# Three feed-forward stages that begin with block products and a plain pair in place of a halved pair

## The chip, the cores and the metric

The kernel runs on one core of one Trainium2 chip. The metric is the device time of one execution in microseconds, lower is better; several executions are run and the median is given. The engines of the core are named as in the profile: PE is TensorE's matmul stream and PEld its weight loads, DVE is VectorE, ACT is ScalarE, POOL is GpSimd, and SP issues most of the transfers.

## The reference

A decoder trunk of two layers over 512 tokens of 1024 features, in float32. Each layer is a half-step feed-forward block, a token mixing block with three branches, and a second half-step feed-forward block, with a root-mean-square norm before and after each. The part that matters here is the feed-forward block, with 2816 hidden features (22 tiles of 128):

```python
def _swiglu(t, w_gate, w_up, w_down):
    return (jax.nn.silu(t @ w_gate) * (t @ w_up)) @ w_down

for l in range(DEPTH):
    f = _swiglu(_rmsnorm(h, ffn1_pre_g[l]), ffn1_w_gate[l], ffn1_w_up[l], ffn1_w_down[l])
    h = h + 0.5 * _rmsnorm(f, ffn1_post_g[l])
    ...
    f = _swiglu(_rmsnorm(h, ffn2_pre_g[l]), ffn2_w_gate[l], ffn2_w_up[l], ffn2_w_down[l])
    h = h + 0.5 * _rmsnorm(f, ffn2_post_g[l])
```

The mixing block also uses the memory, 256 rows of 1024 features, normed by the reciprocal root of each row's mean square.

## The kernel before

**Numbers in two parts.** Every float32 operand of a matmul is split into a high part (`h`, a cast on ScalarE, line 188 or 191) and a low part (`l`, the difference, on VectorE, line 189 or 192). `mm3` then issues three matmuls, high by high, high by low and low by high (lines 214 to 216). So every weight unit of 128 x 1024 elements per use costs one transfer of 512 KB, one cast and one subtraction.

**Stages.** There are four feed-forward stages, `a0`, `c0`, `a1` and `c1`, and between a and c of a layer stands the mixing. Stage `a0` takes the input `x`; the other three take the normed output of the stage before (`src` is b0, c0 and b1). 20 of the 22 hidden tiles are computed in five groups of four (`TG` = 0, 4, 8, 12, 16). A group's gate and up products over the two halves of the tokens and the two halves of the features are computed in a Strassen-like scheme of seven block products instead of eight, each over 128-token stationary blocks with 512 weight columns moving: 24 matmuls of 512 columns (`gate_up`). Products 0 and 1 (and 6) take parts of the normed input itself; 2 to 5 take sums over the halves of the tokens, which VectorE makes (`sums`). Products 0 and 1 need only the first half of the tokens. Group 0 runs in the order 0 to 6 (`FIRST`), the others in the order 0, 2, 3, 4, 5, 1, 6 (`ORDER`). The result of each product is accumulated in a bank and copied or added into a tile, and after product 6 two transposition steps (`feature_major`) turn the group's hidden features.

**The remaining pair.** Hidden tiles 20 and 21 (`EARLY`) are computed as an ordinary pair, gate and up, in the function `halved` (line 808): once over the first half of the tokens, 96 matmuls of 256 columns, and once over the second half, 96 more. A stage begins while the norm of its last two token tiles is still being computed. Therefore its jobs begin: half 0 of the pair, product 0 of group 0, half 1 of the pair, which waits for all tokens, and then products 1 to 6 of group 0, product 0 and 2 of group 4, the transpositions of group 0, and so on. Half 0 of the pair and product 0 cover the norm's last steps.

**The norm and the planner.** The jobs of TensorE are traced in the order of a queue, and beside it run chains: for each token tile the residual, the norm (line 604) and the transposition (line 614, then the split in lines 191 and 192). A planner counts the columns of the matmuls at 2370 a microsecond, and places the steps of a chain by waits in these planner microseconds (line 625): `W_U` plus, where the norm has no other slack (the norms in front of c0, a1 and c1), `W_N` for the token tiles 2 and 3. For the last tile W_U = 5.7 and W_N = 4.0 behind a first wait of 4.8 put the transpositions 14.5 planner microseconds behind the start of the stage.

**Order on the engines.** The framework orders each engine's instructions by its own model of time: what is ready goes first, earlier traced work goes ahead, and only what is pinned (`keep_in_program_order`, or `Q.pinned` in `split`) stays behind all that was traced on its engine. So the order on an engine differs from that of the source.

**Buffers.** Accumulators are eight banks of 128 x 512: four under the tag "mm" and four under "z". Weights pass through four load buffers ("raw") and four buffers each for the high and low parts ("wh", "wl"); the first four units of a stage are split into other tiles ("tri" and `spare`), so that they can be ready before the stage begins. A unit is loaded ahead when its load buffer comes free (`fetch_ahead`). For products 2 and 5 the sum of two weight blocks is formed by a transfer and an accumulating transfer that POOL issues (line 318).

**The memory.** In stage a0 `mem_stats` (line 1081) loads the memory's two tiles of 128 rows, squares and sums the rows, and computes their rates with Ln and Exp (lines 1088 and 1089). `mem_norm`, traced near the end of a0's down products, loads the rows again, scales them (line 1110) and transposes them (line 1116).

Of the kernel before, what the change touches and what calls it, by code (L numbers as in the profile page):

```python
# [17 lines left out]
P = 128  # L18
# [4 lines left out]
def kernel(  # L23
# [217 lines left out]
    class Unit:  # L241
# [46 lines left out]
    class BlockUnit(Unit):  # L288
# [45 lines left out]
        def load(self):  # L334
            if self.h is not None:
                return
            self.fetch()
            if self.twin is not None:
                self.raw = self.twin.raw
            if self.n in self.SUMS:  # L340
                src = self.keep.get(self.SUMS[self.n][0], self.k0)
            elif self.n in (3, 6):
                src = self.keep.get(0, self.k0)
                nc.vector.tensor_tensor(src, src, self.raw[:], ALU.add)
            else:
                src = self.raw[:]
            self.split_from(src)
            if self.raw is not None and not self.lent:
                self.raw = None
                Q.fetched -= 1  # L350
            Q.fetch_ahead()

    class Keep:

# [273 lines left out]


    W_H, W_U = 4.8, (8.0, 7.0, 7.0, 5.7)  # L630
    W_N = (0.0, 0.0, 3.0, 4.0)


    TG = (0, 4, 8, 12, 16)
# [6 lines left out]
    def ffn(l, src, wg, wu, wd, dst, name, spare, aside=None):  # L641
# [4 lines left out]

        hid, st = {}, {}
        hr = {}
        act = lambda k, c=FULL: quad_act(src.us)(k, c)

        def hidden(f, pg, pu):
            s = tmp(f"s{name}_{f}")
            nc.scalar.activation(s[:], pg[:], AF.Silu)
            nc.vector.tensor_tensor(s[:], pu[:], s[:], ALU.mult)
            t = blk("q", f"hid{name}_{f}")
            hid[f] = t[:, 0], t[:, 1]
            split(*hid[f], s[:])
# [150 lines left out]
        def halved(f, ug, uu, half):  # L808
# [21 lines left out]
                            yield (1 + low) * S // 2 * PE_US  # L830
            if half == 1:
                for m in range(2):
                    hidden(f + m, st["p"][m], st["p"][2 + m])

        def down_out(t, hf, pt, seeded):
            if seeded:
# [105 lines left out]
        marks["early"] = ug + uu  # L942
        for un, place in zip(ug + uu, ("tri", "tri", (spare, spare), (spare, spare))):
            un.tags = place
# [12 lines left out]
        some(8)  # L957
        if name == "a0":
            Q.add([], vectors)
            Q.add([], lambda: iter(mem_stats() or ()))  # L960
# [117 lines left out]

    mem_rstd = cst.tile([P, MT, 2], F32, name="mem_rstd")

    def mem_stats():

        for t in range(MT):
            raw, ss = stile([P, D], "rs", f"mst{t}", F32), mem_rstd[:, t]
            nc.sync.dma_start(raw[:], mem[0, t * P:(t + 1) * P, :])
            nc.scalar.activation(raw[:], raw[:], AF.Square, accum_out=ss[:, 0:1])
            nc.vector.tensor_scalar(ss[:, 0:1], ss[:, 0:1], 1.0 / D, EPS, ALU.mult, ALU.add)
            nc.scalar.activation(ss[:, 1:2], ss[:, 0:1], AF.Ln)
            nc.scalar.activation(ss[:, 1:2], ss[:, 1:2], AF.Exp, scale=-0.5)
            nc.vector.tensor_scalar(ss[:, 0:1], ss[:, 0:1], ss[:, 1:2], None, ALU.mult)  # L1090
            nc.vector.tensor_scalar(ss[:, 0:1], ss[:, 0:1], ss[:, 1:2], None, ALU.mult)
            nc.vector.tensor_scalar(ss[:, 0:1], ss[:, 0:1], -0.5, 1.5, ALU.mult, ALU.add)
            nc.vector.tensor_scalar(ss[:, 1:2], ss[:, 1:2], ss[:, 0:1], None, ALU.mult)

    def mem_norm(l, mn):

# [8 lines left out]
        for t in range(MT):  # L1105
            raws.append(stile([P, D], "rs", f"mraw{l}_{t}", F32))
            nc.sync.dma_start(raws[t][:], mem[0, t * P:(t + 1) * P, :])
        yield 0.0
        for t in range(MT):
            nc.vector.tensor_scalar(raws[t][:], raws[t][:], mem_rstd[:, t, 1:2], None, ALU.mult)  # L1110
# [661 lines left out]
```

## Time and profile before

| quantity | value |
| --- | --- |
| median of 3 runs | 2365.17 us (2364.74 to 2366.39) |
| profiled execution | 2364.29 us, span of its instructions 2362.2 us |
| granted clock of TensorE in it | 0.999 |
| start of stages c0, a1, c1 (first matmul of the half pair) | 851.35, 1187.29, 2021.11 us |

In the rows below, times are microseconds from the start of the span. A row of the timeline gives the start, the time from the first start to the last end, the engine, the line, the operation, the written and read tiles, the shape and how many instructions were merged; in square brackets stands the idle time of the engine before and what ended it. Matmuls overlap: one of 512 columns takes 0.39 us from its start to its end, and the next starts long before, so the rate is read from the starts. The number in a tile's name is left out, and the last letter is that of the stage: `pgc` is the gate bank of a c stage, `pta` a block product of an a stage, `us_b` the normed input of stage c0 or c1, `agc` a sum over token halves, `wh_tc` and `wl_tc` a weight unit.

### The profile page before, as it was taken

The page shows a single profiled execution, that of the slowest core. Times are in us where ns is not written, and L with a number is a line of the kernel's source. Part 1 is how long each engine was busy: PE and PEld are TensorE (multiplying, and loading weights), DVE is VectorE, ACT ScalarE, POOL GpSimd, SP SyncE. Part 2 cuts the span into 40 slices and gives each one's busy share as a digit, 9 for nine tenths or more (in the row PEclk, how much of TensorE's full clock was granted, in tenths as well). Part 3 has the DMA queues.
Part 4 walks back from the last instruction along what each step waited for, and adds up shares of the span by engine and source line. Part 5 has one row for each costly group of instructions (what it writes and reads, how often), then busy time and mean ns, then how long its engine had stood idle before and what let it go on. Part 6 is the DMA issues. An engine that isn't in the chain of part 4 may idle for free.

```text
span 2362.2 us, 31098 instructions
## 1 busy us (share of the span) xinstructions
PE 2348.4 (99%) x11656; PEld 1984.4 (84%) x11656; DVE 1778.4 (75%) x2436; ACT 1440.2 (61%) x2329; POOL 213.0 (9%) x242
## 2 busy tenths in 40 slices
PE   9999999999999999999999999999999999999998
PEld 7888888888888898888888888888888888888887
DVE  8766977778776678769787679766787766876696
ACT  6665665577665555566655566656675655555574
POOL 1101100001020001101011110000011100011100
PEclk9999999999999999999999999999999999999999
DMA  8866854222223467759568767632232234686672
GB/s 243 236 173 178 222 187 143 72 72 81 82 71 116 152 196 185 190 159 242 180 179 212 185 187 223 195 102 81 63 90 81 72 127 151 175 228 175 183 218 98
DMA packets 233114, 366.50 MB, mean 155 GB/s; under 512 B 11242, under 2 KB 101634, under 8 KB 232452
## 3 DMA queue, kind: packets, MB, share of 16 engines
q1 hardware_dynamic: 202400, 305.76, 39.5%
q0 software_dynamic: 30560, 58.76, 14.4%
q8 instruction: 91, 1.49, 0.3%
q14 instruction: 59, 0.48, 0.1%
q10 hardware_dynamic: 4, 0.00, 0.0%
HBM read 349.80 MB, written 14.68 MB: 154 GB/s over the span
## 4 chain that ended last, share of the span: by engine, by line
PE 91%; DVE 4%; DMA 2%; ACT 1%; issue 1%; POOL 0%; SPq 0%; DVEq 0%; POOLq 0%; ACTq 0%
PE ptc L216 5%; PE ptc L215 5%; PE ptc L214 5%; PE pta L216 5%; PE pta L214 5%; PE pta L215 5%; PE pg L216 3%; PE pg L214 3%; PE pg L215 3%; PE pdc L216 3%; PE pda L216 3%; PE pdc L214 3%; PE pdc L215 3%; PE pda L215 3%; PE pda L214 3%; PE pb L214 2%
## 5 line engine op out<-in xcount | busy, mean ns | idle before, releaser
L214 PE MATMUL pg<-us_a,wh_wg 128*128 128x512 f32 x384 | 150.9, 393 | 0.0
L216 PE MATMUL pg<-us_a,wl_wg 128*128 128x512 f32 x384 | 149.7, 390 | 0.0
L215 PE MATMUL pg<-us_a,wh_wg 128*128 128x512 f32 x384 | 149.6, 390 | 0.0
L189 DVE TENSOR_TENSOR wl_tc<-ktc,wh_tc 128x1024 fp32r<-128x1024 f32 x80 | 97.4, 1221 | 61.6 <-ACT wh_tc L188 61.5
L189 DVE TENSOR_TENSOR wl_ta<-kta,wh_ta 128x1024 fp32r<-128x1024 f32 x80 | 97.5, 1222 | 56.4 <-ACT wh_ta L188 56.3
L216 PE MATMUL pta<-wh_ta,aga 128*128 128x512 f32 x320 | 124.6, 390 | 0.9 <-DVE aga L189 0.9
L214 PE MATMUL ptc<-wh_tc,agc 128*128 128x512 f32 x320 | 125.2, 391 | 0.0
L214 PE MATMUL pta<-wh_ta,aga 128*128 128x512 f32 x320 | 125.2, 391 | 0.0
L215 PE MATMUL ptc<-wl_tc,agc 128*128 128x512 f32 x320 | 124.5, 389 | 0.0
L215 PE MATMUL pta<-wl_ta,aga 128*128 128x512 f32 x320 | 124.5, 389 | 0.0
L216 PE MATMUL ptc<-wh_tc,agc 128*128 128x512 f32 x320 | 124.5, 390 | 0.0
L188 ACT CAST wh_tc<-ktc 128x1024 fp32r<-128x1024 f32 x80 | 84.0, 1053 | 63.8 <-PE ptc L216 40.8
L188 ACT CAST wh_ta<-kta 128x1024 fp32r<-128x1024 f32 x80 | 84.1, 1053 | 61.3 <-PE pta L216 39.3
L189 DVE TENSOR_TENSOR wl_tc<-raw_tc,wh_tc 128x1024 fp32r<-128x1024 f32 x60 | 73.0, 1222 | 39.6 <-ACT wh_tc L188 39.6
L189 DVE TENSOR_TENSOR wl_ta<-raw_ta,wh_ta 128x1024 fp32r<-128x1024 f32 x60 | 73.1, 1222 | 38.1 <-ACT wh_ta L188 38.1
L215 PE MATMUL ptc<-wl_tc,us_b 128*128 128x512 f32 x240 | 93.6, 390 | 0.0
L214 PE MATMUL ptc<-wh_tc,us_b 128*128 128x512 f32 x240 | 93.5, 391 | 0.0
L216 PE MATMUL ptc<-wh_tc,us_b 128*128 128x512 f32 x240 | 93.1, 389 | 0.0
L188 ACT CAST wh_tc<-raw_tc 128x1024 fp32r<-128x1024 f32 x60 | 62.9, 1052 | 46.8 <-PE ptc L216 40.1
L188 ACT CAST wh_ta<-raw_ta 128x1024 fp32r<-128x1024 f32 x60 | 62.9, 1052 | 43.6 <-PE pta L216 38.3
L216 PE MATMUL pdc<-wh_dc,ac 128*128 128x512 f32 x224 | 87.4, 392 | 0.7 <-DVE ac L189 0.7
L216 PE MATMUL pda<-wh_da,aa 128*128 128x512 f32 x224 | 87.4, 392 | 0.7 <-DVE aa L189 0.7
(533 smaller groups left out, 7414.2 us busy)
## 6 DMA issues: line engine op xcount, KB each, us to landing
raw_wg<-in_w_gate_dram SPq DMA_DIRECT2D x48, 512.0 KB, 3.6
raw_ta<-in_ffn_w_gate_dram SPq DMA_DIRECT2D x44, 512.0 KB, 4.1
raw_tc<-in_ffn_w_gate_dram SPq DMA_DIRECT2D x44, 512.0 KB, 4.6
raw_da<-in_ffn_w_down_dram SPq DMA_DIRECT2D x42, 512.0 KB, 3.8
raw_dc<-in_ffn_w_down_dram SPq DMA_DIRECT2D x42, 512.0 KB, 3.4
kta<-in_ffn_w_up_dram SPq DMA_DIRECT2D x40, 512.0 KB, 6.1
ktc<-in_ffn_w_up_dram SPq DMA_DIRECT2D x40, 512.0 KB, 6.6
raw_wo<-in_w_out_dram SPq DMA_DIRECT2D x24, 512.0 KB, 3.4
```

Source lines behind the costliest of these rows:

```text
L188: both = [nc.scalar.copy(h_ap, src)]
L189: make = lambda: nc.vector.tensor_tensor(l_ap, src, h_ap.bitcast(F32), ALU.subtract)
L214: nc.tensor.matmul(pt, lh, rh, start=start, stop=False, skip_group_check=free)
L215: nc.tensor.matmul(pt, lh, rl, start=False, stop=False, skip_group_check=free)
L216: nc.tensor.matmul(pt, ll, rh, start=False, stop=stop, skip_group_check=free)
```

## The change

In the three stages whose source is not `x`, the jobs now begin with product 0 of group 0, product 1 of group 0 and product 0 of group 4, all on the first half of the tokens; then the pair runs once over all tokens (`plain`, with `both`), gate first and then up, 96 matmuls of 512 columns; then products 2 to 6 of group 0, product 2 of group 4, the transpositions of group 0, and the rest as before. Product 0 of groups 0 and 4 is copied out of its banks into a parked tile; product 1 of group 0 is added to it, and when product 2 begins, ScalarE copies the parked tile back into two "mm" banks, where products 3, 5 and 6 accumulate on. The weights that are split ahead of the stage are now those of group 0's products 0 and 1; the pair's gate weights are split before group 4's product 0 runs, and its up weights before the pair. Stage a0 keeps its halved pair. The last token tile's `W_N` is 2 instead of 4. The memory's squares stay where they were, and its rates are computed in `mem_norm`, for both tiles at once. The accounts of load buffers are kept in one place.

```diff
         def loaded(self):
             self.raw = None
-            if self.ring():
-                Q.fetched -= 1
+            Q.fetched -= self.place == "raw"
             Q.fetch_ahead()
...
-    W_N = (0.0, 0.0, 3.0, 4.0)
+    W_N = (0.0, 0.0, 3.0, 2.0)
...
+        halves = src.name == "x"
...
-        def hidden(f, pg, pu):
+        def silu(f, pg):
             s = tmp(f"s{name}_{f}")
             nc.scalar.activation(s[:], pg[:], AF.Silu)
+            return s
+
+        def hidden(f, s, pu):
             nc.vector.tensor_tensor(s[:], pu[:], s[:], ALU.mult)
...
         def gate_up(f, n, uns, last_of_top):
+            early = f in TG[:2] and not halves
+            if early and n == 2:
+                p0 = st.pop(("p0", f))
+                st["gb", 0] = seeds("mm", f"pt{name}_{f}_0", [p0[:, e] for e in range(2)])
+                if f == TG[1]:
+                    st["c", 0, 0] = p0
             seeded = ("gb", 1) in st if n == 1 else False
             if n in (0, 1, 2) and not seeded:
-                st["gb", SUM[n]] = [pbank("z" if n == 0 and f == TG[0] else "mm", f"pt{name}_{f}_{n}_{e}") for e in range(2)]
+                tag = "z" if halves and n == 0 and f == TG[0] else "mm"
+                st["gb", SUM[n]] = [pbank(tag, f"pt{name}_{f}_{n}_{e}") for e in range(2)]
...
             i, j = TO[n]
+            if early and n == 0:
+                t = st["p0", f] = stile([P, 2, S], "rs", f"c{name}_{f}_00", F32)
+                for e in range(2):
+                    nc.scalar.copy(t[:, e], pts[e][:])
+                return
+            if early and n == 1 and f == TG[0]:
+                t = st["c", 0, 0] = stile([P, 2, S], "f", f"c{name}_{f}_00", F32)
+                for e in range(2):
+                    nc.vector.tensor_tensor(t[:, e], st["p0", f][:, e], pts[e][:], ALU.add)
+                return
...
+        def in_place(units):
+            Q.pinned = True
+            for un in units:
+                un.load()
+            Q.pinned = False
+
+        def after_loading(units, run):
+            def go():
+                in_place(units)
+                yield from run()
+            return go
+
+        def plain(f, ug, uu):
+            in_place(uu)
+            tc.keep_in_program_order(nc.scalar.activation(st["c", 0, 0][:], st["c", 0, 0][:], AF.Silu))
+            next(summed)
+            pg = [pbank("mm", f"pg{name}_{f + m}") for m in range(2)]
+            yield from both(ug, pg)
+            s = [silu(f + m, pg[m]) for m in range(2)]
+            Q.hold, Q.pinned = False, True
+            Q.load_ahead(2)
+            Q.pinned = False
+            next(summed)
+            pu = [pbank("mm", f"pu{name}_{f + m}") for m in range(2)]
+            yield from both(uu, pu)
+            for m in range(2):
+                hidden(f + m, s[m], pu[m])
+
+        def both(uns, pts):
+            for un in uns:
+                for k in range(un.nk):
+                    kk = un.k0 + k
+                    for m, pt in enumerate(pts):
+                        cols = slice(m * P, (m + 1) * P)
+                        mm3(pt[:], un.h[:, k, cols], un.l[:, k, cols], *act(kk), kk == 0, kk == ND - 1, free=True)
+                        yield 3 * S * PE_US
...
-        start = next(todo)
-        Q.add(ug + uu + start[0], lambda: halved(EARLY, ug, uu, 0), src.ready((0, 1)))
-        Q.add([], start[1])
-        Q.add([], lambda: halved(EARLY, ug, uu, 1), src.ready(range(NT)))
+        if halves:
+            start, after = next(todo), None
+            marks["early"] = ug + uu
+            Q.add(ug + uu + start[0], lambda: halved(EARLY, ug, uu, 0), src.ready((0, 1)))
+            Q.add([], start[1])
+            Q.add([], lambda: halved(EARLY, ug, uu, 1), src.ready(range(NT)))
+        else:
+            after = turns(TG[1])
+            start, then, ahead = next(todo), next(todo), next(after)
+            marks["early"] = start[0] + then[0]
+            Q.add(marks["early"] + ahead[0], start[1], src.ready((0, 1)))
+            Q.add([], then[1])
+            Q.add(ahead[0], after_loading(ug, ahead[1]))
+            Q.add(ug + uu, lambda: plain(EARLY, ug, uu), src.ready(range(NT)))
+        for un, place in zip(marks["early"], ("tri", "tri", (spare, spare), (spare, spare))):
+            un.tags = place
         Q.add([], lambda: iter(park() or ()))
         marks["first"] = len(Q.jobs)
         add_sums()
-        some(1)
-        add_sums()
+        if halves:
+            some(1)
+            add_sums()
         some(8)
...
-            todo = turns(g)
-            some(2)
+            todo = after if g == TG[1] and after is not None else turns(g)
+            some(1 if todo is after else 2)
...
-    def mem_stats():
+    def mem_squares():
 
         for t in range(MT):
             raw, ss = stile([P, D], "rs", f"mst{t}", F32), mem_rstd[:, t]
             nc.sync.dma_start(raw[:], mem[0, t * P:(t + 1) * P, :])
             nc.scalar.activation(raw[:], raw[:], AF.Square, accum_out=ss[:, 0:1])
-            nc.vector.tensor_scalar(ss[:, 0:1], ss[:, 0:1], 1.0 / D, EPS, ALU.mult, ALU.add)
-            nc.scalar.activation(ss[:, 1:2], ss[:, 0:1], AF.Ln)
-            nc.scalar.activation(ss[:, 1:2], ss[:, 1:2], AF.Exp, scale=-0.5)
...
+    def mem_rates():
+        a, b = (mem_rstd[:, :, i] for i in range(2))
+        nc.vector.tensor_scalar(a, a, 1.0 / D, EPS, ALU.mult, ALU.add)
+        nc.scalar.activation(b, a, AF.Ln)
+        nc.scalar.activation(b, b, AF.Exp, scale=-0.5)
...
             nc.sync.dma_start(raws[t][:], mem[0, t * P:(t + 1) * P, :])
+        mem_rates()
         yield 0.0
```

More of the change, by code (lines that the diff above doesn't have):

```diff
@@ L348, in load @@
             if self.raw is not None and not self.lent:
-                self.raw = None
-                Q.fetched -= 1
-            Q.fetch_ahead()
+                self.loaded()
+            else:
+                Q.fetch_ahead()
     class Keep:
@@ L832, in halved @@
                 for m in range(2):
-                    hidden(f + m, st["p"][m], st["p"][2 + m])
+                    hidden(f + m, silu(f + m, st["p"][m]), st["p"][2 + m])
+        def in_place(units):
[31 more added lines that the diff above has]
+                        yield 3 * S * PE_US
         def down_out(t, hf, pt, seeded):
@@ L941, in ffn @@
         ug, uu = (wpair(w[l], ND, EARLY * P, f"{x}{name}_{EARLY}") for x, w in (("g", wg), ("u", wu)))
-        marks["early"] = ug + uu
-        for un, place in zip(ug + uu, ("tri", "tri", (spare, spare), (spare, spare))):
-            un.tags = place
         summed = sums()
@@ L947, in ffn @@
         todo = turns(TG[0])
-        start = next(todo)
-        Q.add(ug + uu + start[0], lambda: halved(EARLY, ug, uu, 0), src.ready((0, 1)))
-        Q.add([], start[1])
-        Q.add([], lambda: halved(EARLY, ug, uu, 1), src.ready(range(NT)))
+        if halves:
[4 more added lines that the diff above has]
+            Q.add([], lambda: halved(EARLY, ug, uu, 1), src.ready(range(NT)))
+        else:
+            after = turns(TG[1])
[7 more added lines that the diff above has]
+            un.tags = place
         Q.add([], lambda: iter(park() or ()))
@@ L959, in ffn @@
             Q.add([], vectors)
-            Q.add([], lambda: iter(mem_stats() or ()))
+            Q.add([], lambda: iter(mem_squares() or ()))
         for g in TG[1:]:
-            todo = turns(g)
-            some(2)
+            todo = after if g == TG[1] and after is not None else turns(g)
+            some(1 if todo is after else 2)
             over, later[:] = later[1:], later[:1]
@@ L1086, in mem_stats @@
             nc.scalar.activation(raw[:], raw[:], AF.Square, accum_out=ss[:, 0:1])
-            nc.vector.tensor_scalar(ss[:, 0:1], ss[:, 0:1], 1.0 / D, EPS, ALU.mult, ALU.add)
[L1088 to L1093, printed above, removed]
+    def mem_rates():
[3 more added lines that the diff above has]
+        nc.scalar.activation(b, b, AF.Exp, scale=-0.5)
+        nc.vector.tensor_tensor(a, a, b, ALU.mult)
+        nc.vector.tensor_tensor(a, a, b, ALU.mult)
+        nc.vector.tensor_scalar(a, a, -0.5, 1.5, ALU.mult, ALU.add)
+        nc.vector.tensor_tensor(b, b, a, ALU.mult)
     def mem_norm(l, mn):
```

## The prediction

> **What bounds the kernel now.** I read the page first (busy shares, the chain that ended last), then who keeps TensorE waiting, and last the stretches in which the three changed stages begin.
>
> ```profile
> span 2362.2 us, 31098 instructions
> PE 2348.4 (99%) x11656; PEld 1984.4 (84%) x11656; DVE 1778.4 (75%) x2436; ACT 1440.2 (61%) x2329; POOL 213.0 (9%) x242
> ...
> PE 91%; DVE 4%; DMA 2%; ACT 1%; issue 1%; POOL 0%; SPq 0%; DVEq 0%; POOLq 0%; ACTq 0%
> ```
>
> TensorE is busy 99% of the span and is 91% of the chain. So time moves only if TensorE issues its work closer together, or if it comes to wait. What 256 and 512 columns cost stands in the table of stretches (length, then busy time and instructions of each engine):
>
> ```profile
> core 0: us, PE busy (x) PEld busy (x) DVE busy (x) ACT busy (x) POOL busy (x), PEclk, DMA share, GB/s
> 843.18:851.35 8.17, 8.17 (x38) 6.76 (x37) 6.61 (x12) 4.43 (x10) 0.28 (x1) 1.00 0.75 238
> 851.35:862.86 11.51, 11.51 (x98) 11.51 (x97) 6.73 (x14) 4.06 (x12) 2.11 (x2) 1.00 1.00 281
> 859.40:863.40 4.00, 4.00 (x36) 4.00 (x35) 0.00 (x0) 0.00 (x0) 0.00 (x0) 1.00 1.08 291
> 870.12:881.63 11.51, 11.51 (x97) 11.51 (x96) 11.51 (x11) 7.91 (x10) 1.06 (x1) 1.00 0.79 184
> 870.34:911.70 41.36, 41.36 (x228) 35.82 (x227) 41.33 (x42) 25.28 (x29) 3.22 (x3) 1.00 0.57 149
> 1206.04:1217.55 11.51, 11.51 (x97) 11.51 (x96) 11.51 (x11) 7.91 (x10) 0.00 (x0) 1.00 0.37 99
> 2039.88:2051.39 11.51, 11.51 (x97) 11.50 (x96) 11.51 (x11) 7.91 (x10) 0.55 (x1) 1.00 0.78 183
> ```
>
> The first row holds 36 matmuls of 512 columns, with the tails of two earlier ones in its count: 8.17/36 = 0.2269 us each. The rows of 11.51 us are the half pairs of stages c0, a1 and c1: 96 matmuls of 256 columns each, so 0.1199 us, where half of 0.2269 would be 0.1135. In these rows the weight load column is as full as the matmul column; in the 512 row it is not (6.76 of 8.17). The clock is 1.00 in all of them.
>
> **The pair.** Each of the three stages gives up two half pairs, 2 x 11.51 = 23.02 us, for one pair of 96 matmuls over 512 columns, 96 x 0.2269 = 21.78 us. The block products are only moved: the start product, product 1 and group 4's product 0 have 24 matmuls of 512 columns wherever they stand. That is 1.24 us a stage, -3.7 us in all.
>
> The Trainium skill ("TensorE: Matmul & The Clock Gate", section "Back-to-back issue gap") gives an isolated warm gap of N/2.4 + 2.5 ns, so an estimate of 109 ns for 256 columns and 216 ns for 512. By that rule two narrow matmuls cost 2.5 ns more than a wide one and the three stages save an estimate of 0.7 us only, which speaks against the change. The trace shows 119.9 and 226.9 ns, a difference of 12.9 ns, and the trace decides.
>
> **A stall that may go.** In each of the three stages TensorE hangs once in product 4, where the stage's saturated VectorE is late (0.02 us idle in the 41.36 us row above).
>
> ```profile
> 898.66 0.39 PE L215 MATMUL ptc<-wl_tc,agc 128*128 128x512 f32 x1
> 899.05 0.73 PE L216 MATMUL ptc<-wh_tc,agc 128*128 128x512 f32 x2
> 899.62 0.39 PE L214 MATMUL ptc<-wh_tc,agc 128*128 128x512 f32 x1
> ...
> 2068.81 0.73 PE L216 MATMUL ptc<-wh_tc,agc 128*128 128x512 f32 x2
> ```
>
> From 898.66 to 899.62 are three matmuls in 0.96 us; at 0.2269 they take 0.68, so 0.27 is lost. Behind the change the splits of the gate weights and the additions of product 1 fall before the second half of the tokens, where VectorE had nothing to do (0.00 in 859.40:863.40). VectorE then has about 2 x 1.14 + 1.28 = 3.6 us less to do (rows below) by product 4. I take -0.27 a stage, -0.8 in all; the ends are -0.8 and 0.
>
> **Two handovers of accumulators.** There are four "mm" banks. Product 2 now needs four at once: two are filled from the parked product 0, two are its own, and the latter are the plain pair's "up" banks, which VectorE still has to read. Then product 2 of group 4 follows product 6 of group 0 directly, and its own banks are those that ScalarE's Silu has yet to read. Before, a product of 24 x 0.2269 = 5.4 us stood in both gaps. Nothing like it stands in the trace, so I bound it by the instructions that must run.
>
> ```profile
> 881.69 1.28 DVE L654 TENSOR_TENSOR sc<-puc,sc 128x512 f32<-128x512 f32 x2
> 882.89 1.21 DVE L678 TENSOR_TENSOR rc<-rc,rc 128x1024 f32<-128x1024 f32 x1
> ...
> 914.98 0.39 PE L216 MATMUL ptc<-wh_tc,us_b 128*128 128x512 f32 x1
> 915.66 0.61 PE L216 MATMUL ptc<-wh_tc,us_b 128*128 128x512 f32 x2
> ...
> 915.40 0.60 ACT L740 ACTIVATE cc<-ptc 128x512 f32<-128x512 f32 x1 [0.98 <-PE ptc L216]
> 916.64 1.05 ACT L188 CAST wh_tc<-ktc 128x1024 fp32r<-128x1024 f32 x1 [0.64 <-DMA ktc<-in_ffn_w_gate_dram]
> 917.59 0.59 ACT L740 ACTIVATE cc<-ptc 128x512 f32<-128x512 f32 x1
> ```
>
> The first bank's last matmul starts 4 x 0.227 = 0.91 us before the product ends and takes 0.39, so it is done 0.52 before the end. Silu started 0.03 after such an end (914.98 + 0.39 = 915.37).
>
> At the first handover VectorE needs 0.64 per bank (1.28 for two), so TensorE waits at least 0.64 + 0.03 - 0.52, some 0.2 us. If VectorE has just begun an operation of 1.21 it is 1.4. What is queued behind on TensorE is product 2 and all after it; but product 3 works on the other two banks, and if its first matmuls are put ahead, nothing is lost. So 0 to 1.4; I take 0.3, near the lower end, as the multiplication at 881.69 came at once in a stage whose VectorE was full. Three stages: +0.9.
>
> At the second, Silu takes 0.60: 0.60 + 0.03 - 0.52 = 0.1 us at best. In this trace the second Silu stood behind a cast that waited 0.64 us for its transfer, and ended at 918.18, 2.3 us after the end of product 6 (915.66 + 0.22, two merged in that row); its bank is needed 0.68 into the product, so 1.6 at worst. TensorE has other work for it:
>
> ```profile
> 909.61 0.27 PE L765 MATMUL thc<-ident,cc 128*128 128x128 f32 x1
> ...
> 925.64 1.36 PE L765 MATMUL thc<-ident,cc 128*128 128x128 f32 x11
> ```
>
> The first row is a transposition of group 0 drawn forward to the start of product 6, three products ahead of the others at 925.64; these others can fill such a gap. 0 to 1.6; I take 0.1, +0.3 in all.
>
> **The second half of the tokens.** The last four transpositions of the norm now come two planner microseconds earlier, and the plain pair wants all tokens, low parts too, with its second matmul (the half pair wanted them after 16).
>
> ```profile
> 858.06 1.28 DVE L604 SCALAR_TENSOR_TENSOR fb<-hm,nhb,gqb 128x1024 f32<-128x1024 f32 x1
> 867.87 1.03 PE L614 MATMUL utb<-ident,fb 128*128 128x128 f32 x8
> 868.50 1.09 ACT L191 ACTIVATE us_b<-utb 128x512 fp32r<-128x512 f32 x2 [3.92 <-PE utb L614]
> 869.13 1.29 DVE L192 SCALAR_TENSOR_TENSOR us_b<-utb,us_b 128x512 fp32r<-128x512 f32 x2 [3.72 <-ACT us_b L191]
> 872.61 2.35 DVE L189 TENSOR_TENSOR wl_tc<-raw_tc,wh_tc 128x1024 fp32r<-128x1024 f32 x2
> ```
>
> The planner counts 0.648 us for three matmuls that take 0.68, so 12.5 planner microseconds after the stage's start are 18 threes and one earlier turn of 0.8: 851.35 + 12.25 + 0.8 = 864.4. The normed rows are there at 859.3. From start of transposition to first low part it took 869.13 + 0.65 - 867.87 = 1.9 us, so 866.3, or 869.9 if the 3.6 us named above stand in front. The pair starts after 24 threes and two turns, 851.35 + 16.3 + 1.7 = 869.4. I take 0, hidden by product 0 of group 4, and 0 to 1.2 (one VectorE operation) as ends. The gate weights must be split by then too; they are issued behind one more pair of loads on SP's queue.
>
> ```profile
> 842.05 1.23 DVE L189 TENSOR_TENSOR wl_uc<-raw_uc,wh_uc 128x1024 fp32r<-128x1024 f32 x1
> ...
> raw_tc<-in_ffn_w_gate_dram SPq DMA_DIRECT2D x44, 512.0 KB, 4.6
> ```
>
> The last unit of the early four is split at 842.05 + 1.23, and with it a load buffer comes free; two gate loads from there, one after the other at 4.6 us, land at 852.5, and at twice that at 861.7, ahead of 869.4. The up weights follow a pair later and are wanted 10.9 us later. Product 0's copies out of the banks, product 1's addition and the Silu were there before. What is new on ScalarE, four copies of 0.6 us a stage into banks, lie in an engine that is 61% busy; without that cover they are 2.4 us a stage.
>
> **The memory's rates.**
>
> ```profile
> 65.46 1.28 ACT L1088 ACT_TABLE_LOAD   x1
> 67.07 1.28 ACT L1089 ACT_TABLE_LOAD   x1
> ...
> 73.08 0.39 PE L215 MATMUL pta<-wl_ta,us_x 128*128 128x512 f32 x1
> 73.48 0.50 PE L214 MATMUL pta<-wh_ta,us_x 128*128 128x512 f32 x1
> 73.82 0.39 PE L215 MATMUL pta<-wl_ta,us_x 128*128 128x512 f32 x1
> ...
> 74.01 0.74 DVE L1110 TENSOR_SCALAR mraw<-mraw,mem_rstd 128x1024 f32<-128x1024 f32 x1
> 317.74 0.60 PE L1116 MATMUL mt<-ident,mraw 128*128 128x128 f32 x4
> ```
>
> Ln and Exp break into the Silu stretch of stage a0 with table loads, and TensorE loses some 0.3 us in the rows beside it (0.74 for two, against 0.45). The step is traced some 200 us later now, but the scaling that stands there already ran at 74.01, 244 us ahead of its use: what is ready is drawn forward. So I expect the rates to run early again (7 in 10), and take 0; ends -0.4 and +0.6 (another such place). That the move does nothing is thus part of the forecast.
>
> **The sum.** -3.7 - 0.8 + 0.9 + 0.3 + 0 + 0 = -3.3 us. The profiled execution took 2364.29 us, which gives 2361.0; it lies 0.9 under the median of the runs, 2365.17, which gives 2361.9. All lower ends together are -4.9, all upper ends -3.7 + 4.2 + 4.8 + 3.6 + 0.6 = +9.5.
>
> **Rivals.** (1) The handovers cost what the pair gains: 0.8 and 0.7 a stage, halfway between their ends, so 3 x 1.5 - 4.5 = 0: 2365.2. For it: VectorE full from 870.34 on. Against: the prompt multiplication. (2) Slower: both handovers at their upper ends because VectorE or ScalarE has an operation, or the cast of a late weight, in front of the reading; 3 x 3.0 - 4.5 = +4.5, and some of the late low parts with it: 2370. It decides from 1.5 us a stage on. For it: the Silu at 917.59. Against: the transpositions and product 3 as fillers. (3) Nothing new waits and a0's losses go as well: -4.9, 2360.3. Against: the handover's 0.2 us. (4) The half pair's 12.9 ns per couple do not come from the narrow matmuls but from something that stays with the pair, such as new weights for every matmul: gain 0, -0.8 + 1.2 = +0.4, 2365.6. Against it stands the first row, where the weights change with every matmul too, at 226.9 ns. The Trainium skill's rule above points the same way, with its estimate of 0.7 us in place of 0.
>
> **How the numbers follow.** Forecast 0.47; (1) 0.22; (2) 0.18; (3) 0.10; (4) 0.03. A measurement tells about 0.2% (4.7 us) from no change: under 2360.4 lie (3) and a tenth of the forecast, 0.15; over 2369.9 lies (2), 0.18; between them is the rest, 0.67. The range reaches from (3) to (2), 2359.8 to 2370.5; the forecast's own is 2360 to 2364.
>
> **What would show it.** No 256-column matmul is left where the three stages begin, and each plain pair takes 21.8 us. TensorE's spacing at the first matmul of product 2, in groups 0 and 4, shows the two handovers: under 0.4 us lost at each if I am right, 1.5 a stage or more if (2) is. No loss at the pair's start, and none in product 4. Two table loads for Ln and Exp before 240 us show the rates drawn forward. It is wrong if a plain pair takes over 22.5 us, or if a weight lands late.

## The result and the profile after

The changed kernel takes 2360.43 us (median of 21 runs, 2359.58 to 2363.19), beside 2364.74 us for the kernel before (21 runs, 2362.87 to 2367.19): a ratio of 0.9984, with a 95% interval of 0.9977 to 0.9991. That is 4.3 us by the medians, and 2 to 5 us by the interval. The profiled execution took 2360.91 us, its span is 3.0 us shorter.

The page of the changed kernel, first part:

```profile
span 2359.2 us, 30541 instructions
...
PE 2346.2 (99%) x11368; PEld 1970.5 (84%) x11368; DVE 1781.2 (75%) x2431; ACT 1445.6 (61%) x2339; POOL 212.5 (9%) x242
```

There are 288 matmuls fewer (3 x 96), and TensorE is still busy 99% of the span. Where the time came from is read from the table of stretches of the changed kernel: first the plain pair of c0 (the other two take the same 21.76 us), then stage c0 from its first matmul to its first down product (a1 and c1 take 222.57 and 222.58).

```profile
869.10:890.86 21.76, 21.76 (x97) 18.03 (x96) 21.69 (x20) 13.04 (x17) 3.60 (x3) 1.00 0.82 212
851.00:1073.60 222.60, 222.51 (x1025) 184.78 (x1024) 160.29 (x160) 130.44 (x177) 28.60 (x24) 1.00 0.71 190
```

Stage c0 of the kernel before (a1 and c1 took 223.48 and 223.50):

```profile
851.35:1074.85 223.50, 223.50 (x1122) 189.84 (x1120) 159.36 (x160) 128.61 (x173) 28.49 (x24) 1.00 0.69 187
```

Each stage is 0.90 to 0.92 us shorter, 2.73 in all. The remaining 0.3 us of the span lie in stage a0. They can't be put down to the change: in two executions of the changed kernel a0's first down product began at 238.45 and at 237.74 us, so such a difference comes and goes without any edit. The rest of the 4.3 us by the medians is only partly found. 0.3 us lie outside the span of instructions: the time exceeds the span by 1.72 us in the changed kernel and by 2.04 us in the kernel before (medians of 21 runs, and of 31 runs beside a later repeat), and why was not looked into. For the last 1.0 us or so there is no trace: one trace of the kernel before was kept.

The plain pair starts without a wait and takes 21.76 us, 1.26 less than the two half pairs. So 0.9 a stage is what is left of 1.26 plus the stall in product 4. The places where it was given back are seen in the timeline of the changed kernel. First, product 2 of group 0 behind the pair:

```profile
890.86 0.39 PE L214 MATMUL ptc<-wh_tc,agc 128*128 128x512 f32 x1
...
891.54 0.70 PE L214 MATMUL ptc<-wh_tc,agc 128*128 128x512 f32 x2
892.09 0.39 PE L215 MATMUL ptc<-wl_tc,agc 128*128 128x512 f32 x1
...
891.01 1.28 DVE L657 TENSOR_TENSOR sc<-puc,sc 128x512 f32<-128x512 f32 x2
```

The four matmuls from 890.86 to 891.54 belong to product 3; product 2 begins with the second of the two in the merged row. VectorE frees the first "up" bank at 891.7, and two matmuls at 0.227 each took 0.55 (892.09 - 891.54): 0.10 is lost.

Then the end of group 0, where product 6 follows product 5 and product 2 of group 4 follows product 6 (TensorE, then VectorE, then ScalarE):

```profile
912.50 0.39 PE L216 MATMUL ptc<-wh_tc,agc 128*128 128x512 f32 x1
912.74 0.49 PE L785 MATMUL thc<-ident,cc 128*128 128x128 f32 x3
913.31 0.47 PE L214 MATMUL ptc<-wh_tc,us_b 128*128 128x512 f32 x1
913.62 0.39 PE L215 MATMUL ptc<-wl_tc,us_b 128*128 128x512 f32 x1
...
918.64 0.40 PE L216 MATMUL ptc<-wh_tc,us_b 128*128 128x512 f32 x1
918.88 0.27 PE L785 MATMUL thc<-ident,cc 128*128 128x128 f32 x1
919.04 0.50 PE L214 MATMUL ptc<-wh_tc,agc 128*128 128x512 f32 x1
919.38 0.40 PE L215 MATMUL ptc<-wl_tc,agc 128*128 128x512 f32 x1
...
920.53 0.69 PE L214 MATMUL ptc<-wh_tc,agc 128*128 128x512 f32 x2
921.05 0.40 PE L215 MATMUL ptc<-wl_tc,agc 128*128 128x512 f32 x1
...
912.48 1.28 DVE L764 TENSOR_TENSOR cc<-cc,ptc 128x512 f32<-128x512 f32 x2
...
918.39 0.60 ACT L760 ACTIVATE cc<-ptc 128x512 f32<-128x512 f32 x1 [0.94 <-PE ptc L216]
919.12 1.05 ACT L188 CAST wh_tc<-ktc 128x1024 fp32r<-128x1024 f32 x1
920.08 0.59 ACT L760 ACTIVATE cc<-ptc 128x512 f32<-128x512 f32 x1
```

Reading: from start to start a wide matmul takes 0.227 and a transposition 0.104 (16 of them in 1.66 us, in a row of the fourth experiment below). From 912.50 to 913.62 stand two wide matmuls and three transpositions, 0.77, in 1.12: 0.35 lost. Of this 0.08 lies behind the first wide matmul (913.31 to 913.62 is 0.31): a wide matmul that comes behind a wait or a transposition is followed in turn only after 0.31 to 0.34 us, in place of 0.227 (here, and at 919.04 and 909.64 below). Product 6 accumulates in the banks of product 5, and the first matmul comes when VectorE's addition has read the first of them, at 913.1 (912.48 + 0.64). From 918.64 to 919.38: 0.56 of work in 0.74, 0.18 lost, most of it again behind the first matmul (0.34 to the next); the first matmul of product 2 comes when the Silu is done (918.39 + 0.60 = 918.99). From 920.53 to 921.05: 0.07 lost behind the second Silu, which stood behind a cast. Together 0.60 a stage. In the kernel before, the first of these places looked like this:

```profile
909.15 0.62 PE L214 MATMUL ptc<-wh_tc,us_b 128*128 128x512 f32 x2
...
909.64 0.47 PE L215 MATMUL ptc<-wl_tc,us_b 128*128 128x512 f32 x1
909.95 0.39 PE L216 MATMUL ptc<-wh_tc,us_b 128*128 128x512 f32 x1
910.18 0.40 PE L215 MATMUL ptc<-wl_tc,us_b 128*128 128x512 f32 x1
```

The five matmuls from 909.15 to 910.18 that read `us_b` are not product 6 yet. They are product 0 of group 4, drawn forward into the gap while VectorE read the banks of product 5, and nothing was lost. The change runs that product long before, so the gap has only transpositions to fill it.

The memory's rates did run early again (ScalarE, changed kernel), and in product 4 nothing is lost any more:

```profile
64.87 1.28 ACT L1162 ACT_TABLE_LOAD   x1
...
66.38 1.28 ACT L1163 ACT_TABLE_LOAD   x1
```

The sum for stage c0 is then -1.26 (pair) - 0.28 (product 4) + 0.10 + 0.60 = -0.84, of -0.90 measured; the other 0.06 was not traced.

### The profile page after: what moved, and what is told of

The parts are those of the page before. It is cut to its first block, busy times and chain, and to the rows that moved or that the text cites. A ratio compares the mean times of both kernels' runs of the same rounds, so it can differ in the third digit from the quotient of the medians.

```text
span 2359.2 us, 30541 instructions
## 1 busy us (share of the span) xinstructions
PE 2346.2 (99%) x11368; PEld 1970.5 (84%) x11368; DVE 1781.2 (75%) x2431; ACT 1445.6 (61%) x2339; POOL 212.5 (9%) x242
## 4 chain that ended last, share of the span: by engine, by line
PE 92%; DVE 5%; issue 1%; ACT 1%; DMA 1%; POOL 0%; SPq 0%; DVEq 0%; POOLq 0%
PE ptc L214 5%; PE ptc L216 5%; PE ptc L215 5%; PE pta L214 5%; PE pta L215 5%; PE pta L216 5%; PE pg L216 3%; PE pg L214 3%; PE pg L215 3%; PE pdc L216 3%; PE pda L216 3%; PE pdc L214 3%; PE pdc L215 3%; PE pda L215 3%; PE pda L214 3%; PE pb L214 2%
## 5 line engine op out<-in xcount | busy, mean ns | idle before, releaser
L216 PE MATMUL pdc<-wh_dc,ac 128*128 128x512 f32 x224 | 87.5, 392 | 0.7 <-DVE ac L189 0.7
L216 PE MATMUL pda<-wh_da,aa 128*128 128x512 f32 x224 | 87.4, 392 | 0.7 <-DVE aa L189 0.7
L214 PE MATMUL ptc<-wh_tc,us_b 128*128 128x512 f32 x224 | 87.7, 392 | 0.2
L214 PE MATMUL pda<-wh_da,aa 128*128 128x512 f32 x224 | 87.6, 391 | 0.0
L214 PE MATMUL pdc<-wh_dc,ac 128*128 128x512 f32 x224 | 87.6, 391 | 0.0
```

The source lines that it names most:

```text
L214: nc.tensor.matmul(pt, lh, rh, start=start, stop=False, skip_group_check=free)
L216: nc.tensor.matmul(pt, ll, rh, start=False, stop=stop, skip_group_check=free)
```

## The experiments

Each is an edit of the changed kernel. Stage lengths are those of the stretch from the first matmul to the first down product, 222.60, 222.57 and 222.58 us in the changed kernel. The first four experiments ran on one chip, without the changed kernel beside them.

### Is it the narrow matmuls?

```diff
-                        mm3(pt[:], un.h[:, k, cols], un.l[:, k, cols], *act(kk), kk == 0, kk == ND - 1, free=True)
+                        for c in HALVES:
+                            mm3(pt[:, c], un.h[:, k, cols], un.l[:, k, cols], *act(kk, c), kk == 0, kk == ND - 1, free=True)
```

> The changed kernel, with every 512-column matmul of the plain pair issued as two of 256 columns, in the same place and order. If the narrow matmuls themselves are what the half pair paid for (119.9 ns each against 226.9 ns for a wide one), each of the three pairs takes 192 x 0.1199 = 23.0 us in place of 21.8, and the time is 3.7 us above the changed kernel's, about 2364.1 us. If the 12.9 ns a couple stay with the pair for another reason (rival 4), the pair takes what it takes now, 21.8 us, and the time stays at 2360.4 within 0.5.

The two halves of a bank are opened separately here, one while the other is being accumulated, and the pair's hidden features are not those of the reference; why was not tried. For the time only this counts: each wide matmul is two narrow ones, 192 in place of 96, in the same place.

```profile
867.59:890.62 23.03, 23.03 (x193) 23.03 (x192) 22.52 (x21) 13.13 (x16) 3.60 (x3) 1.00 0.76 198
```

The pair takes 23.03 us, as two half pairs did (2 x 11.51 = 23.02), and stage c0 takes 223.95 us, 1.35 longer. 2365.43 us, against 2364.0 for the kernel before on the same chip (ratio 1.0007, 0.9998 to 1.0016). The narrowness alone is the price: 1.27 us a pair, and rival 4 is out. The order and the place of the pair were left alone. What it is in a narrow matmul that costs this was not separated: the weight loads fill the narrow pair (23.03 of 23.03 us) and not the wide one (18.03 of 21.76). The ratio stands 0.0023 above the changed kernel's 0.9984, 5.4 us where 3.7 were expected; in the profiled execution c0's down products, which the edit does not touch, lost 1.3 us more than in the changed kernel (see the last section); whether they did so in the median run is not shown.

### The rates, moved back or pinned

The second experiment puts the rates beside the squares again, as before the change. The third keeps them late:

```diff
-        nc.scalar.activation(b, a, AF.Ln)
-        nc.scalar.activation(b, b, AF.Exp, scale=-0.5)
+        tc.keep_in_program_order(nc.scalar.activation(b, a, AF.Ln))
+        tc.keep_in_program_order(nc.scalar.activation(b, b, AF.Exp, scale=-0.5))
```

> The changed kernel, with the memory's rates computed beside its squares again, tile by tile, as before the change. Theory: the move of the rates does nothing by itself, since they are drawn forward in both; the time is that of the changed kernel, 2360.4, within 0.3. Rival: the 0.33 us by which stage a0 became shorter (its first down product began at 238.78 before and at 238.45 after) come from the move, so the time is 0.3 us longer, the first down product begins at 238.8, and the loss near 73 us has its old form.

> The changed kernel, with Ln and Exp of the memory's rates kept behind all that was traced on ScalarE before them, so that they cannot be drawn forward. Theory: the two table loads at 64.87 and 66.38 us and the one back at 77.72 go, and with them the delay of the Silus behind which TensorE loses some 0.6 us near 60 and 72 us; the time is 0.3 to 0.6 us under the changed kernel's, 2359.8 to 2360.1, and a0's first down product begins by 238.1. Rival: the losses near 72 us have another cause, and the late rates delay the memory's transpositions: the time is the same or up to 1 us longer.

Back: 2361.05 us, ratio to before 0.9986 (0.9977 to 0.9995), the table loads again at 64.28 and 65.89. Pinned: 2360.8 us, 0.9985 (0.9976 to 0.9994). Neither can be told from the changed kernel by its time, though both medians lie above what the theories gave, by 0.35 and 0.7 us. With the rates back, a0's first down product began at 237.63 us, so the rival's 238.8 did not come. The trace of the pinned one shows the loads gone, Ln and Exp at 298.54 and 298.77 us without one, and TensorE near 72 us thus, changed kernel first:

```profile
72.14 0.49 PE L214 MATMUL pta<-wh_ta,us_x 128*128 128x512 f32 x1
72.88 0.50 PE L215 MATMUL pta<-wl_ta,us_x 128*128 128x512 f32 x1 [0.24 <-DVE wl_ta L189]
```

```profile
72.36 0.50 PE L214 MATMUL pta<-wh_ta,us_x 128*128 128x512 f32 x1
72.69 0.39 PE L215 MATMUL pta<-wl_ta,us_x 128*128 128x512 f32 x1
```

0.74 between two matmuls became 0.33, so 0.4 us at this place is due to the early rates (0.3 by a second execution of the changed kernel, where it was 0.65). The path is not the one that was expected, ScalarE's table loads and the Silus: the row names VectorE. There the scaling of the memory's rows, which early rates let run early, took 0.75 us from 70.94, right before the subtraction that TensorE waited for, 71.61 to 72.83. The move as such did nothing that shows, as the second experiment says: a later place in the source is not a later place on the engine. The pinned version did not reach the 0.3 us less that the theory named; its execution lost 0.7 us near 60 us, where the changed kernel lost 0.5 and other executions nothing.

### Copying the parked product back later

```diff
-            if early and n == 2:
+            if early and n == 3:
                 p0 = st.pop(("p0", f))
                 st["gb", 0] = seeds("mm", f"pt{name}_{f}_0", [p0[:, e] for e in range(2)])
```

> The changed kernel, with the parked product 0 copied back into banks when product 3 begins instead of when product 2 begins, in groups 0 and 4. Theory: in the changed kernel the early copies of group 4 take the banks that product 4 had freed, and product 2 gets those that the Silu of product 6 still reads; copied later, they leave the free banks to product 2, whose first matmuls can then also fill the gap between products 5 and 6 of group 0. The losses between 912 and 921 us (0.33 + 0.08 + 0.14 + 0.11 + 0.07 beyond regular spacing) go but for one return from transpositions of 0.09, and so does the 0.09 us at product 2 of group 0: 0.6 to 0.7 us a stage, the time 2358.3 to 2358.7. Rival: it is VectorE's addition of product 5 and the order of casts on ScalarE that keep TensorE waiting, whichever bank is taken: then at most 0.2 us a stage, 2359.8 or more; and a copy that now comes too late for product 3 would make it longer than 2360.4.

```profile
849.56:1071.49 221.93, 221.93 (x1025) 184.81 (x1024) 160.19 (x160) 130.40 (x177) 27.56 (x23) 1.00 0.71 190
```

Stage c0 takes 221.93 us, a1 and c1 221.94 each: 0.63 to 0.67 us less, the theory's 0.6 to 0.7. The timeline shows the place between products 5 and 6 of group 0, and the transpositions, now in one piece:

```profile
911.64 0.49 PE L214 MATMUL ptc<-wh_tc,us_b 128*128 128x512 f32 x1
911.97 0.39 PE L215 MATMUL ptc<-wl_tc,us_b 128*128 128x512 f32 x1
...
922.20 1.91 PE L785 MATMUL thc<-ident,cc 128*128 128x128 f32 x16
923.86 0.48 PE L214 MATMUL ptc<-wh_tc,agc 128*128 128x512 f32 x1
```

0.33 instead of 0.227 at 911.64, 0.10 lost, and nothing at product 2 of either group. By the banks that the built program gives each tile (the profile leaves out the number), product 2 of group 0 now has the pair's "gate" banks, free since the Silu, and the copies have the "up" banks. In the order of TensorE's instructions two matmuls of product 2 of group 4 now stand ahead of product 6, as those of product 0 did in the kernel before. So nearly all of the 0.70 that the changed kernel lost at the handovers was a matter of the order: the copies were ready early, were put early, and took the banks that a product could have used.

The time was 2359.1 us, ratio to before 0.9979 (0.9970 to 0.9988), 0.4 above the expected band. The interval overlaps that of the changed kernel, 0.9977 to 0.9991, so the gain stands on the stretches. In the profiled execution c0's down products lost 2.5 us (last section); whether that explains the 0.4 in the median is not shown.

### What the cover is worth, and the last tile (the changed kernel beside them: 2360.25 us, ratio 0.9981, 0.9972 to 0.9990)

> The changed kernel itself, so that the next kernels have it beside them on one chip. Expected: some 0.16% under the kernel before, 2360.4 us in the earlier runs; each c and a1 stage takes 222.6 us from its first block product to its first down product.

It came out as that: 222.59 us for c0's stretch.

```diff
-            Q.add(ahead[0], after_loading(ug, ahead[1]))
-            Q.add(ug + uu, lambda: plain(EARLY, ug, uu), src.ready(range(NT)))
+            Q.add(ug + uu, after_loading(ug, lambda: plain(EARLY, ug, uu)), src.ready(range(NT)))
+            Q.add(ahead[0], ahead[1])
```

> The changed kernel with product 0 of group 4 behind the plain pair in place of ahead of it. Theory: that product is what hides the norm of the last two token tiles; without its 5.4 us the pair's first low parts are 4 to 5 us late, nothing is at hand to fill the gap, and each of the three stages loses 3 to 5 us: 2370 to 2375 us. On the other side product 0 of group 4 stands again between the pair and product 2. Rival: VectorE and ScalarE had the low parts ready long before and the order alone was free: 2360 to 2362 us.

```profile
860.70 1.91 PE L613 MATMUL utb<-ident,fb 128*128 128x128 f32 x16
862.96 0.73 PE L214 MATMUL pgc<-us_b,wh_gc 128*128 128x512 f32 x2 [0.35 <-ACT us_b L191]
863.90 0.50 PE L215 MATMUL pgc<-us_b,wh_gc 128*128 128x512 f32 x1 [0.21 <-DVE us_b L192]
```

And the last transpositions in the changed kernel:

```profile
865.50 1.03 PE L613 MATMUL utb<-ident,fb 128*128 128x128 f32 x8
```

2364.52 us, ratio 1.0002 (0.9993 to 1.0011): without the cover the gain is gone. The direction was right, the size was not. Each stage loses 1.2 us (223.74 against 222.60), not 3 to 5, and it is lost at the pair's start: 0.60 before 862.96, 0.49 before 863.90 and 0.11 behind. The transpositions of both token tiles now come in one piece, the last eight some 11.7 us behind the start of the stage (860.70 + 8 x 0.104 - 849.81), against 14.50 in the changed kernel (865.50 - 851.00), and VectorE splits at once. So product 0 of group 4 hides 1.2 us with 5.4 us of work; the rest of it is margin.

```diff
-    W_N = (0.0, 0.0, 3.0, 2.0)
+    W_N = (0.0, 0.0, 3.0, 4.0)
```

> The changed kernel with W_N = 4 for the last token tile, as before the change. In the changed kernel the last low parts are ready at 868.6 us and the pair's second row of matmuls wants them at about 869.3. Two planner microseconds later, the last transpositions fall into the end of product 0 of group 4, their low parts are ready at 870.5 to 871.5, and each stage loses 1 to 2 us at the pair's start: 2363.5 to 2366.5. Rival: the framework's order hides it (only the high parts are wanted first): within 0.5 us of 2360.4.

```profile
867.15 1.03 PE L613 MATMUL utb<-ident,fb 128*128 128x128 f32 x8
...
868.72 0.61 PE L214 MATMUL pgc<-us_b,wh_gc 128*128 128x512 f32 x2
869.21 0.50 PE L215 MATMUL pgc<-us_b,wh_gc 128*128 128x512 f32 x1
```

2360.69 us, ratio 0.9983 (0.9974 to 0.9992); the rival came out. The last transpositions come 16.54 us behind the start of the stage (867.15 - 850.61), 2.0 later than in the changed kernel, and the pair loses 0.15, 0.04 before 869.21 and 0.11 behind it: its first two matmuls, one for each bank, are put ahead and are high by high only, and the first low part is there when they are done, at about 869.1 (VectorE's split began at 868.47). The smaller wait is worth 0.1 us a stage at the most.

### What took the stall out of product 4

```diff
             tc.keep_in_program_order(nc.scalar.activation(st["c", 0, 0][:], st["c", 0, 0][:], AF.Silu))
+            idle = st["p0", TG[0]]
+            for _ in range(3):
+                tc.keep_in_program_order(nc.vector.scalar_tensor_tensor(idle[:], idle[:], 1.0, idle[:], ALU.mult, ALU.max))
             next(summed)
```

> The changed kernel with three more VectorE operations (a tile times one, its larger with itself, some 1.28 us each, 3.8 us in all) pinned ahead of the sums over token halves, in each of the three stages. Theory of the prediction: the stall in product 4 went because VectorE had 3.6 us less to do by then, so 3.8 us more bring it back, 0.2 to 0.4 us a stage between 896 and 901 us. Rival: it went because the last sums over token halves, which product 4 needs, are now made during the plain pair; they end at 889.96 and are wanted at 898, 8 us later, in the kernel before they ended at 898.99. Then 3.8 us move them to about 894 and nothing is lost in product 4; what can be lost is at product 2's start, where VectorE's reading of the pair's up banks comes later: 0 to 1.4 us.

> The same with seven such operations, 9.0 us in all. Theory of the prediction: the stall in product 4 is larger than the 0.27 us of before, by some 5 us. Rival: the margin of 8 us is used up, so 0.5 to 1.5 us are lost in products 2 to 4, and the stage is that much longer than 222.6 us.

The second kernel has seven operations in place of three. There is one execution of each, 2360.9 and 2363.61 us. An operation took 1.22 us and the next instruction began 1.14 behind it, so they are 3.4 and 8.0 us of VectorE's time, somewhat less than expected. With three nothing is lost in product 4; the three stages take 222.99, 222.73 and 222.64 (0.29 of the 0.39 more in c0 are lost in product 2 of group 4). With seven the stages take 223.65, 223.65 and 223.63; nothing is lost in product 4 either, but product 2 waits:

```profile
890.54 0.70 PE L214 MATMUL ptc<-wh_tc,agc 128*128 128x512 f32 x2
892.24 0.50 PE L214 MATMUL ptc<-wh_tc,agc 128*128 128x512 f32 x1 [1.00 <-DVE sc L657]
...
890.37 1.21 DVE L192 SCALAR_TENSOR_TENSOR agc<-rc,agc 128x1024 fp32r<-128x1024 f32 x1
891.50 1.28 DVE L657 TENSOR_TENSOR sc<-puc,sc 128x512 f32<-128x512 f32 x2
```

That is the forecast's first handover near its upper end: 1.25 us, with an operation of 1.21 in front of the reading; it needed 8 us of extra work on VectorE to appear. And for product 4 the traces speak for the rival. The low parts of the sums for products 4 and 5 (line 189, `agc`; the first is product 4's) were made here, in the kernel before, in the changed one (product 4's alone), with three operations more and with seven more:

```profile
897.78 2.34 DVE L189 TENSOR_TENSOR agc<-rc,agc 128x1024 fp32r<-128x1024 f32 x2
```

```profile
886.47 1.22 DVE L189 TENSOR_TENSOR agc<-rc,agc 128x1024 fp32r<-128x1024 f32 x1
```

```profile
893.89 2.35 DVE L189 TENSOR_TENSOR agc<-rc,agc 128x1024 fp32r<-128x1024 f32 x2
```

```profile
901.85 2.35 DVE L189 TENSOR_TENSOR agc<-rc,agc 128x1024 fp32r<-128x1024 f32 x2
```

Before, the first of the two ended at 899.0 and TensorE wanted it at 898.9 to 899.1. In the changed kernel product 4 begins 48 matmuls behind the pair, 890.86 + 48 x 0.227 + 0.1 = 901.9 (not 898, as the expectation had it), and the low part is there at 886.47 + 1.22 = 887.7: 14 us of margin. With three operations more it is there at 895.1 and product 4 begins at 901.4, so 6 us of margin are left although VectorE has nearly all of the 3.6 us to do again. With seven it is there at 903.1 and its first use starts at 903.47: 0.4 us are left, and nothing is lost. No run put the sums back behind the pair, so that their earlier place is enough by itself is read from these traces and was not tried.

### Both edits together

> The changed kernel with both edits: the parked product copied back when product 3 begins, and Ln and Exp kept in place on ScalarE. If the two gains add, it takes 1.9 us less by the three stages (3 x 0.64, seen in the stages of the first) and some 0.4 us less in a0 (the loss near 72 us, gone with the second alone): 2.3 us under the changed kernel's time on the same chip. Rival: the down products of c0 lost 2.6 us in the profile of the first edit, in place of 0.5, because their transfers land no earlier when the stage ends earlier; if that is so in most runs, only 0.3 to 1.0 us remain.

```profile
849.79:1071.75 221.96, 221.96 (x1026) 184.86 (x1024) 160.19 (x160) 130.39 (x177) 27.56 (x23) 1.00 0.71 190
```

2358.54 us (2357.32 to 2360.28), ratio to before 0.9973 (0.9963 to 0.9983), beside 2360.25 and 0.9981 for the changed kernel on the same chip. It is the lowest median of all. The stages take 221.96, 221.94 and 221.97 us, as with the one edit alone. The difference of 1.7 us to the changed kernel stands on the medians and on the stretches; the two intervals to the kernel before overlap. It is 0.6 short of the 2.3 expected, of which c0's down products took some 0.5 in the profiled execution.

## Why the prediction was right, and where not

The forecast was 2361.9 us, -3.3 us against the kernel before; measured were 2360.43 and -4.3, with an interval that holds -3.3. By the profiled stages the forecast was -1.11 each, and -0.90 to -0.92 were measured. So the three stages, which the sum was made of, gave 2.73 us and less than the 3.3, and the medians moved by more, through 1.6 us outside of these stages that the sum did not have. That the time came so near is in part luck. Point by point:

- **The pair, -1.24 a stage.** Measured -1.26 (21.76 against 23.02), and the first experiment, which gave 23.03 for the same pair in narrow matmuls, shows the reason. The Trainium skill's rule for an isolated matmul ("TensorE: Matmul & The Clock Gate", section "Back-to-back issue gap") would have made it an estimate of 0.7 us for all three; the runs show 1.27 for one.
- **Product 4, -0.27 a stage.** The size was right (0.28) and the reason wrong, so this term came out by luck. It is not the 3.6 us that VectorE had less to do by then: 3.4 and 8.0 us of extra work did not bring the stall back. By the traces it is the order, since the sums are now made beside the plain pair.
- **First handover, +0.3.** Measured +0.10. The mechanism was as written, with product 3's first matmuls put ahead; the term was too large by 0.2. It and the 0.25 at product 2 of group 4 are each under the 0.4 that the prediction named as its sign.
- **Second handover, +0.1.** This is the step that failed: 0.60 were measured, inside the bounds of 0 to 1.6. Of it, 0.25 are the two waits for Silu that the step named (0.18 and 0.07), so the transpositions that it counted on were weak fillers: one 0.104 us long was used. The other 0.35 lie between products 5 and 6, a place that the prediction did not name. It counted product 0 of group 4 as cover for the gap behind product 6; the same product had been filling the gap in front of it too.
- **Second half of the tokens, 0.** Right, with less room than was worked out. The last transpositions came 14.50 us behind the start of the stage, where 13.05 was forecast (864.4 - 851.35), and the first low part was there at 868.55 (VectorE's split began at 867.91), 0.8 before its first use at 869.33 and not 3. Ahead of them stood 20 threes and the earlier turn (20 x 0.68 + 0.8 = 14.4), not 18: 20 threes are 12.96 planner microseconds, so the planner evidently did not count the turn in its 12.5, where the working did count it. Without the cover the step would cost 1.2 us a stage, and the wait of the last tile, W_N, hardly matters.
- **The memory's rates, 0, drawn forward.** Right: table loads at 64.87 and 66.38. The lower end, -0.4, was of the right size, since pinning them saves 0.3 to 0.4 us at that place in a0; the time does not show it, and the upper end was not tried.
- **Rivals.** (1) and (2) needed 1.5 us and more of handovers a stage; there were 0.7. (3), nothing waits, did not come: 0.7 us a stage waited. That the median, 2360.43, lies near its 2360.3 does not speak for it: the three stages give 2.73 us and not the 4.5 that it needs of them. (4) fell with the first experiment.

## What to carry to other kernels

When a piece of work is moved, ask which gaps it was filling where it stood: a scheduler may have been using its first instructions in two places, and only one of them is the gap that the source shows. A copy that is ready early takes a buffer early; traced one step later, it left the free banks to the product that needed them, and gave 0.65 us a stage without any work saved. Moving the rates' lines in the source moved nothing on ScalarE, whose instructions the framework puts by what is ready; only pinning did.

## What was not expected of the hardware

A gain in front of a place that is bound by transfers may not reach the end. In the fourth experiment stage c0's down products began 2.1 us earlier than in the changed kernel (1071.49 against 1073.60), and here ScalarE and TensorE waited:

```profile
1085.86 1.05 ACT L188 CAST wh_dc<-btc 128x1024 fp32r<-128x1024 f32 x1 [2.39 <-DMA btc<-in_ffn_w_down_dram]
...
1092.30 0.50 PE L216 MATMUL pdc<-wh_dc,ac 128*128 128x512 f32 x1 [1.63 <-DVE ac L189]
```

And the same places in the changed kernel:

```profile
1085.78 1.05 ACT L188 CAST wh_dc<-btc 128x1024 fp32r<-128x1024 f32 x1 [0.20 <-DMA btc<-in_ffn_w_down_dram]
...
1092.33 0.74 PE L216 MATMUL pdc<-wh_dc,ac 128*128 128x512 f32 x2 [0.34 <-DVE ac L189]
```

The cast of the same weight began at the same moment, the wait for it grew from 0.20 to 2.39 us, and stage a1 began at 1185.99 us, against 1186.05: the lead of 2.1 us was gone. It did not happen in all executions: between two matmuls there, 1.8 us were lost in the first experiment too, 1.0 with both edits, 0.9 without the cover, and 0.5 in the others. Why the transfers land later in some was not tried and stays open.
